# Hyena filters in fewer, wider VectorE operations, and w_out's copy in DRAM issued in the first batch

## The chip, the cores and the metric

One core of one Trainium2 chip. Its engines are TensorE (PE for matmuls, PEld for its weight loads), VectorE (DVE), ScalarE (ACT), GpSimd (POOL) and SyncE (SP, which only issues DMAs here). The metric is the device time of one execution in microseconds (us), lower is better; a kernel's time is the median over its runs.

## The reference, cut to what matters

An encoder layer on two inputs of 1024 tokens × 1024 channels (x_prompt and x_sample), which share all weights. A Fourier branch and a Hyena branch are gated and merged. The Hyena branch multiplies, twice in a row, by a long convolution, whose filter kf is computed from a small network:

```python
    h = (h @ w3.astype(f32)).reshape(L, N_DIR, H_ORDER, H_WIDTH)
    h = h * jnp.exp(-t[:, None, None, None] * jnp.abs(decay.astype(f32))[None])
    h = h / jnp.sum(jnp.abs(h), axis=(0, 1), keepdims=True)
    k = jnp.concatenate([h[:, 0],
                         jnp.zeros((1, H_ORDER, H_WIDTH), f32),
                         h[:L - 1, 1][::-1]], axis=0)
    return jnp.fft.rfft(k, axis=0)
...
    for n, gate in enumerate((x1, x2)):
        z = gate.astype(jnp.float32) * long_conv(z, kf[:, n],
                                                 hyena_d[n].astype(jnp.float32))
    y_h = (z.astype(dt) * jax.nn.silu(hg)) @ w_hyena_out
...
    out = (g_f * y_f + g_h * y_h) @ w_out
    return x + rmsnorm(out, g_post)
```

`x @ w_in` gives all projections (v, x1, x2 and the gates). The filters do not depend on the input, so there are 2 orders × 8 column tiles = 16 of them, computed once and used by both batches.

## The kernel before, in words

**Precision.** Every large product is split: an operand is held as a rounded part and a rest (`wh`/`wl`, `xh`/`xl`, `bh`/`bl`), and one product is three matmuls (`mm3`). All matmuls through `mm` carry line 194 in the profile; DVE and POOL arithmetic through helpers carries lines 177 (`stt`, scalar-tensor-tensor) and 181 (`add`, `sub`, `mul`, the rest of a split), and casts of a split carry line 171.

**Stages.** A Fourier phase runs from 0 to about 250 us. Then come the sixteen filters, between about 230 and 710 us, with gate projections (`spill_gate`) laid between them so that PE has work. Then `branches` runs 32 steps, 16 for each batch, until about 1770 us. The rest, `phase_blocks`, holds the output projections.

**One filter.** `filter_taps` takes column tile ct of order n. For each m of 4 and each i of 2 it makes two matmuls into half of a PSUM tile `pft` (256 columns), an Exp on ACT into `ex` (L640), a product on DVE into `T[i][:, m]`, and an Abs on ACT (L643) into `ex` or, for m = 0, `acc`. DVE adds the Abs values up into `acc`, folds them twice, and a matmul with ones (`pn`, L652 and L653) sums over the partitions. `T0` holds the even row blocks (i = 0), `T1` the odd ones. `filter_spectrum` forms `fE = T0 + T1` and `fO = T0 − T1` (128x1024 each), folds them into `xp` and `xm`, and hands these to `butterfly`, which makes four 128x512 pieces b0 to b3 and splits them into `bh` and `bl`. `forward` multiplies a piece by a table into PSUM (`pXf`). From each group's result DVE and ACT make eight blocks of `kt` (L680 to L698), which SP stores in DRAM as `d_k` (L701, L703).

**The first batch's weights.** `inproj` needs `w_in` in chunks of 128x512 in two parts. SP loads `wr` (L757), ACT casts it to the rounded part (L761) and writes its negative (L762), and POOL issues a DMA that adds the original onto the negative (L763), which leaves the rest. The handle of that DMA is `self.added`. Four places ("rooms") take turns: two pairs `wh`/`wl`, and two tiles `whl` in buffers named draw and draw2. The parts of the three Hyena sections are kept: POOL stores each pair in DRAM as `d_w` (L736), which waits until the accumulating DMA has landed. One chunk serves 24 matmuls `pin`.

**Branches.** Step i computes the projections of step i + 1 and transforms them (`conv_front`, `butterfly`, with the same tile for xp and xm), and then runs `conv_back` for step i: `forward` into `pX`, a product with `k`, loaded from `d_k` by SP (L833) into the two buffers that the filters' `kt` used, giving `t` and `y`, and the inverse transform (`pT`). In the first batch the gate `sg` of a step is read back and passed through Silu on ACT (L1013). In the second batch the weights are read from `d_w` (SP, L754), and a generator, `staging`, advances through POOL: it loads into the rooms draw and draw2, folds, and stores. It waits for `tick`, written by ACT. In its rounds with q = 1 it also issued a transfer in DRAM, eight in all, that brings `w_out` into the layout `d_wo`:

```python
paced = nc.gpsimd.tensor_copy(r[:, 0::2, 0:1], self.tick)
if q == 1:
    i, w = half, (k + 4 * half) * P
    with self.tc.issue_after(paced.ins):
        nc.gpsimd.dma_start(self.d_wo[:, k, 2 * i:2 * i + 2], ...)
```

**Order.** The code is written in the order above, but a scheduler fixes each engine's instruction order at build time, from its own estimates of how long things take. The hardware then keeps that order on each engine and waits where data or a buffer is late.

## Time and profile before

| | |
|---|---|
| time, median of 3 runs | 2428.06 us (2427.44 to 2429.68) |
| profiled execution | 2431.53 us, of which the span is 2429.8 us |
| granted TensorE clock over the span | 0.992 of full |
| busy: PE, DVE, ACT, POOL | 2367.3, 1994.0, 1161.3, 451.1 us |
| DVE in 1250 to 1400 and 1400 to 1550 us | 141.2 and 149.5 of 150 us |
| ACT table loads of 1.28 us, 677 to 693 us | 4 |
| d_wo's transfers issued | 8, of 512 KB each, 1239.2 to 1352.6 us |

A profile is one execution, so its times are a little apart from the median. In lists of waits the columns are the total, the count and the longest; in timelines they are the start, the duration, engine, line, operation and the tiles written and read, and in brackets how long the engine was idle before the instruction and what ended that. Tables by stage give, for each stretch, its length, the busy time of each engine with its instructions, the granted clock, the share of the DMA engines and GB/s.

### The profile page before, as it was taken

The numbers are of one execution on the slowest core, as the hardware profiler recorded it, in microseconds if no ns is written. First come the engines' busy times: TensorE is split into PE (matmuls) and PEld (weight loads), VectorE is DVE, ScalarE is ACT, GpSimd is POOL, SyncE is SP. The second block draws the span as 40 slices with busy tenths as digits, with TensorE's granted clock in tenths as the row PEclk, the third lists the DMA queues.
The fourth block names the chain that finished last, engine by engine and source line by source line (L and its number), as shares of the span: only waits on it lengthen the run. The fifth ranks groups of instructions, "written<-read, shape, count | busy, mean of one in ns | idle before, by whom it ended". The sixth has DMA issues, their size and how long they took to land. (4 is left out here: it accounts for less than half of the span.)

```text
span 2429.8 us, 37269 instructions
## 1 busy us (share of the span) xinstructions
PE 2367.3 (97%) x13006; PEld 2055.2 (85%) x13006; DVE 1994.0 (82%) x3856; ACT 1161.3 (48%) x2208; POOL 451.1 (19%) x575
## 2 busy tenths in 40 slices
PE   6999899999999999999999999999999999999998
PEld 5998788888888888888888888888878888888786
DVE  7785777877777999999899999997666687777777
ACT  5545666666664444444222232333344375656543
POOL 1331111111122222222024554320000000101000
PEclk9999999999999999999999999999999999999999
DMA  7536777887778677766366766554546687888744
GB/s 276 189 124 220 193 197 212 221 212 201 212 218 229 187 201 206 195 184 202 127 225 195 233 210 211 190 174 134 208 149 227 213 300 252 271 269 228 223 157 155
DMA packets 265012, 499.65 MB, mean 206 GB/s; under 512 B 26662, under 2 KB 92423, under 8 KB 264568
## 3 DMA queue, kind: packets, MB, share of 16 engines
q1 hardware_dynamic: 220076, 380.53, 47.9%
q0 software_dynamic: 44560, 116.72, 18.9%
q8 instruction: 102, 1.67, 0.3%
q14 instruction: 86, 0.70, 0.1%
q10 hardware_dynamic: 188, 0.02, 0.0%
HBM read 333.59 MB, written 167.77 MB: 206 GB/s over the span
## 5 line engine op out<-in xcount | busy, mean ns | idle before, releaser
L194 PE MATMUL pin<-xh,wl 128*128 128x512 f32 x1024 | 401.0, 393 | 2.5 <-DMA wl<-d_w 2.5
L194 PE MATMUL pin<-xl,wh 128*128 128x512 f32 x1024 | 402.6, 393 | 0.0
L194 PE MATMUL pin<-xh,wh 128*128 128x512 f32 x1024 | 401.5, 393 | 0.9 <-DMA wh<-d_w 0.9
L194 PE MATMUL pin<-xh,whl 128*128 128x512 f32 x896 | 293.5, 397 | 2.3 <-DMA whl<-in_w_in 2.3
L194 PEld LDWEIGHTS pin<-xh,wl 128*128 128x128 f32 x1024 | 193.4, 189 | 37.9 <-DMA wl<-d_w 2.9
L194 PEld LDWEIGHTS pin<-xh,wh 128*128 128x128 f32 x1024 | 193.3, 189 | 36.5 <-DMA wh<-d_w 1.3
L194 PEld LDWEIGHTS pin<-xl,wh 128*128 128x128 f32 x1024 | 193.4, 189 | 34.4
L194 PEld LDWEIGHTS pin<-xh,whl 128*128 128x128 f32 x896 | 167.6, 190 | 35.5 <-DMA whl<-in_w_in 2.5
L194 PE MATMUL pT<-cinv,yh 128*128 128x256 f32 x1024 | 193.1, 283 | 0.0
L194 PE MATMUL pin<-xl,whl 128*128 128x512 f32 x448 | 177.2, 396 | 0.0
L194 PEld LDWEIGHTS pT<-cinv,yh 128*128 128x128 f32 x1024 | 165.1, 191 | 9.1
L181 DVE TENSOR_TENSOR t<-pX,k 128x1024 f32<-128x1024 f32 x128 | 155.7, 1216 | 13.2 <-PE pX L194 6.2
L194 PE MATMUL pX<-bh,cfwd 128*128 128x256 f32 x768 | 160.8, 286 | 4.2 <-DVE t L181 3.6
L171 ACT CAST yh<-y 128x512 fp32r<-128x512 f32 x128 | 79.3, 619 | 170.1 <-DVE y L181 139.1
L194 PE MATMUL pT<-cinv,yl 128*128 128x256 f32 x512 | 145.7, 285 | 0.0
L171 ACT CAST bh<-b 128x512 fp32r<-128x512 f32 x144 | 88.7, 618 | 98.4 <-DVE b L181 61.2
L194 PEld LDWEIGHTS pX<-bh,cfwd 128*128 128x128 f32 x768 | 126.3, 191 | 8.1 <-DVE t L181 3.9
L181 POOL TENSOR_TENSOR draw<-draw 128x256 f32<-128x256 f32 x96 | 101.7, 1059 | 129.8 <-DMA draw<-d_g 49.9
L181 DVE TENSOR_TENSOR bl<-b,bh 128x512 fp32r<-128x512 f32 x144 | 104.1, 724 | 23.1 <-ACT bh L171 22.9
L194 PE MATMUL pX<-bl,cfwd 128*128 128x256 f32 x384 | 109.9, 286 | 1.4 <-DVE bl L181 1.4
L181 DVE TENSOR_TENSOR yl<-y,yh 128x512 fp32r<-128x512 f32 x128 | 91.0, 711 | 11.1 <-ACT yh L171 10.9
L194 PEld LDWEIGHTS pT<-cinv,yl 128*128 128x128 f32 x512 | 98.1, 192 | 2.0 <-DVE yl L181 0.2
(368 smaller groups left out, 6071.3 us busy)
## 6 DMA issues: line engine op xcount, KB each, us to landing
k<-d_k SPq DMA_DIRECT2D x128, 512.0 KB, 4.4
wr<-in_w_in SPq DMA_DIRECT2D x136, 256.0 KB, 3.3
d_g<-gt SPq DMA_DIRECT2D x92, 256.0 KB, 3.3
d_k<-kt SPq DMA_DIRECT2D x128, 128.0 KB, 3.0
d_k<-kt SPq DMA_DIRECT2D x64, 256.0 KB, 3.5
fz<-d_g SPq DMA_DIRECT2D x64, 256.0 KB, 5.1
wl<-in_w_in POOLq DMA_DIRECT2D x56, 256.0 KB, 5.3
whl<-in_w_in POOLq DMA_DIRECT2D x56, 256.0 KB, 5.4
```

The costliest lines, as they stand in the source:

```text
L171: self.rounded = nc.scalar.copy(h, src)
L181: return e.tensor_tensor(out, a, b, op=op)
L194: return self.nc.tensor.matmul(out, lhsT, rhs, start=start, stop=stop, skip_group_check=shared)
```

## The change

In the filters, each operation works on both halves i of an m, or on both blocks of a pair:

- `T` is laid out by m // 2 instead of by i, so that the product and the Abs take 128x512 at once: 4 of each per filter instead of 8 (the Exp stays at 8).
- `fE` and `fO` are formed in two halves of 128x512 each: first the half of m = 2 and 3, which `db` doesn't enter, then the other.
- `butterfly` writes b1's first two blocks in one operation for filters; for the convolutions two of its operations swap places.
- In the three groups with g ≠ 0, `kt` takes two `stt` of 128x256 instead of one of 128x256 and two of 128x128.
- The eight transfers of `w_out` leave `staging` and stand in steps 1 to 8 of `branches`, each issued by POOL after the last accumulating weight DMA.

```diff
@@ -583,9 +583,12 @@
             de, do, sgn = sm[:, 0, 1], sm[:, 1, 1], 1.0
             se, so = sm[:, 0, 0], sm[:, 1, 0]
         e0, o0, e2, o2 = xm[:, 0, 0], xm[:, 1, 0], xm[:, 0, 2], xm[:, 1, 2]
-        self.stt("dve", b1[:, 0], de, C8, e0)
+        if xm is xp:
+            self.stt("dve", b1[:, 0], de, C8, e0)
+            self.stt("dve", b1[:, 1], se, C8, e2)
+        else:
+            self.stt("dve", b1[:, 0:2], sm[:, 0, ::-1], C8, xm[:, 0, 0:3:2])
         self.stt("dve", b1[:, 3], do, C8 * sgn, o0)
-        self.stt("dve", b1[:, 1], se, C8, e2)
         self.stt("dve", b1[:, 2], so, -C8, o2, MUL, SUB)
         split(1, b1)
         self.stt("dve", b3[:, 0], de, -C8, e0)
@@ -627,7 +630,7 @@
         dec = ws.tile([P, 256], F32, tag="dec", name="dec", bufs=1)
         nc.sync.dma_start(dec, a["filt_decay"][n, ct].partition_broadcast(P))
         nc.scalar.activation(dec, dec, AF.Abs)
-        T = [ws.tile([P, 4, 2, P], F32, tag="x", name=f"T{i}", bufs=4) for i in range(2)]
+        T = [ws.tile([P, 2, 2, 2, P], F32, tag="x", name=f"T{i}", bufs=4) for i in range(2)]
         acc = ws.tile([P, 2, 2, P], F32, tag="yl", name="acc", bufs=2)
         accf = acc.rearrange("p a d c -> p a (d c)")
         for m in range(4):
@@ -638,9 +641,9 @@
                 self.mm(ps[:, i], self.hid[:, q * P:(q + 1) * P], w3h, True, False)
                 self.mm(ps[:, i], self.hid[:, q * P:(q + 1) * P], w3l, False, True)
                 nc.scalar.activation(ex[:, i], dec, AF.Exp, scale=self.vec[:, q:q + 1])
-                Tm = T[i][:, m].rearrange("p d c -> p (d c)")
-                self.mul("dve", Tm, ps[:, i], ex[:, i])
-                nc.scalar.activation(accf[:, i] if m == 0 else ex[:, i], Tm, AF.Abs)
+            Tm = T[m // 2][:, m % 2].rearrange("p i d c -> p i (d c)")
+            self.mul("dve", Tm, ps, ex)
+            nc.scalar.activation(accf if m == 0 else ex, Tm, AF.Abs)
             if m:
                 self.add("dve", accf, accf, ex)
         db = ws.tile([P, P], F32, tag="db", name="db", bufs=1)
@@ -653,16 +656,17 @@
         nc.tensor.matmul(pn[:, P:P + 2], sm, self.ones[:, 0:2], start=True, stop=True)
         nc.vector.reciprocal(self.invn[:, n * 8 + ct:n * 8 + ct + 1], pn[:, P:P + 1])
         self.mul("dve", db, pn[:, 0:P], db)
-        self.stt("dve", T[1][:, 0, 0], db, self.vec[:, 9:10], T[1][:, 0, 0])
-        nc.vector.tensor_scalar(T[0][:, 3, 1], T[0][:, 3, 1], self.vec[:, 8:9], None, op0=MUL)
+        self.stt("dve", T[0][:, 0, 1, 0], db, self.vec[:, 9:10], T[0][:, 0, 1, 0])
+        nc.vector.tensor_scalar(T[1][:, 1, 0, 1], T[1][:, 1, 0, 1], self.vec[:, 8:9], None, op0=MUL)
         return T
 
     def filter_spectrum(self, n, ct, T, ws):
         nc = self.nc
         E = ws.tile([P, 4, 2, P], F32, tag="t4", name="fE", bufs=2)
         O = ws.tile([P, 4, 2, P], F32, tag="t4", name="fO", bufs=2)
-        self.add("dve", E, T[0], T[1])
-        self.sub("dve", O, T[0], T[1])
+        for h in (1, 0):
+            self.add("dve", E[:, 2 * h:2 * h + 2], T[h][:, :, 0], T[h][:, :, 1])
+            self.sub("dve", O[:, 2 * h:2 * h + 2], T[h][:, :, 0], T[h][:, :, 1])
         xp = ws.tile([P, 2, 4, P], F32, tag="q", name="xp", bufs=2)
         xm = ws.tile([P, 2, 4, P], F32, tag="u", name="xm", bufs=1)
         self.add("dve", xp[:, 0], E[:, :, 0], E[:, ::-1, 1])
@@ -679,9 +683,8 @@
 
                 nc.scalar.activation(tmp, X, AF.Copy, scale=th(0))
                 self.stt("dve", kt[:, 0:6:5], X[:, :, 1], th(1), tmp[:, :, 0])
-                self.stt("dve", kt[:, 2], X[:, 1, 0], th(4), tmp[:, 1, 1])
-                self.stt("dve", kt[:, 4], X[:, 0, 0], th(1), tmp[:, 0, 1], MUL, SUB)
-                nc.scalar.mul(kt[:, 1:4:2], kt[:, 0:4:2], -1.0)
+                self.stt("dve", kt[:, 4:2:-1], X[:, :, 0], th(1), tmp[:, :, 1], MUL, SUB)
+                nc.scalar.mul(kt[:, 1:3], kt[:, 0:4:3], -1.0)
             else:
                 for i, pr in enumerate(pairs):
                     R, I = X[:, i, 0], X[:, i, 1]
@@ -965,11 +968,7 @@
                     r = self.stage2.tile([P, 4, 256], F32, tag="draw2", name="draw", bufs=1)
                 else:
                     r = self.cp.tile([P, 4, 256], F32, tag="draw", name="draw", bufs=1)
-                paced = nc.gpsimd.tensor_copy(r[:, 0::2, 0:1], self.tick)
-                if q == 1:
-                    i, w = half, (k + 4 * half) * P
-                    with self.tc.issue_after(paced.ins):
-                        nc.gpsimd.dma_start(self.d_wo[:, k, 2 * i:2 * i + 2], a["w_out"][w:w + P].rearrange("p (n c) -> p n c", n=2))
+                nc.gpsimd.tensor_copy(r[:, 0::2, 0:1], self.tick)
                 for i in range(2):
                     src = {1: self.d_g[0][0], 2: self.d_sh[0]}[q][k + 4 * i] if q < 5 else a["w_out"][(k + 4 * i) * P:(k + 4 * i + 1) * P]
                     nc.gpsimd.dma_start(r[:, 2 * i:2 * i + 2], src.rearrange("p (n c) -> p n c", n=2)[:, :, s])
@@ -1022,6 +1021,10 @@
                 gates(i + 1)
                 if i + 2 < len(steps) and steps[i + 2][0] != steps[i + 1][0]:
                     self.load_x(steps[i + 2][0])
+            if 0 < i <= 8:
+                k, h, w = (i - 1) % 4, (i - 1) // 4, (i - 1) * P
+                with tc.issue_after(self.added.ins):
+                    nc.gpsimd.dma_start(self.d_wo[:, k, 2 * h:2 * h + 2], self.a["w_out"][w:w + P].rearrange("p (n c) -> p n c", n=2))
             y = self.conv_back(n, c, B, ws, stage if b else None)
             B = nxt
             for _ in range({4: 2, 3: 2, 2: 2, 1: 2}.get(len(steps) - i, 0)):
```

Over the whole program DVE has 96 instructions fewer, and ACT five table loads instead of nine. The scheduler's order differs on all engines from about 250 us on; on PE it is the same again from about 1700 us.

**First place: the first filter, about 250 to 270 us.** DVE, with the first filter's acc (acc_3001) and the last pieces of the Fourier phase (fA_2895, fB_2896); first before, then changed:

```order
L657 TENSOR_SCALAR T0_2999<-T0_2999,vec_68 128x128
L181 TENSOR_TENSOR acc_3001<-acc_3001,ex_3028 128x512
L177 SCALAR_TENSOR_TENSOR fA_2895<-pQ_2922,vec_68,fPs_2929 128x255
L181 TENSOR_TENSOR fB_2896<-pQ_2922,fPm_2930 128x255
L177 SCALAR_TENSOR_TENSOR fA_2895<-pQ_2922,vec_68,fPs_2929 128x254
L177 SCALAR_TENSOR_TENSOR fB_2896<-pQ_2922,vec_68,fPm_2930 128x254
L181 TENSOR_TENSOR T1_3000<-pft_3040,ex_3041 128x256
L181 TENSOR_TENSOR w3s_3095<-w3_3092,w3s_3095 128x256
L181 TENSOR_TENSOR acc_3001<-acc_3001,ex_3041 128x512
L181 TENSOR_TENSOR acc_3001<-acc_3001 128x256
L181 TENSOR_TENSOR acc_3001<-acc_3001 128x128
L654 RECIPROCAL invn_72<-pn_3057 128x1
```

```order
L181 TENSOR_TENSOR T1_3000<-pft_3034,ex_3035 128x512
L181 TENSOR_TENSOR w3s_3087<-w3_3084,w3s_3087 128x256
L181 TENSOR_TENSOR acc_3001<-acc_3001,ex_3035 128x512
L660 TENSOR_SCALAR T1_3000<-T1_3000,vec_68 128x128
L181 TENSOR_TENSOR acc_3001<-acc_3001 128x256
L181 TENSOR_TENSOR acc_3001<-acc_3001 128x128
L177 SCALAR_TENSOR_TENSOR fA_2895<-pQ_2902,vec_68,fPs_2909 128x258
L181 TENSOR_TENSOR fB_2896<-pQ_2902,fPm_2910 128x258
L177 SCALAR_TENSOR_TENSOR fA_2895<-pQ_2902,vec_68,fPs_2909 128x258
L177 SCALAR_TENSOR_TENSOR fB_2896<-pQ_2902,vec_68,fPm_2910 128x258
L657 RECIPROCAL invn_72<-pn_3049 128x1
L181 TENSOR_TENSOR db_3045<-pn_3049,db_3045 128x128
```

Before, the group of pQ_2902 stood five rows ahead of these and that of pQ_2922 between the adds. Now all adds of acc stand ahead of both groups, and the group of pQ_2902 lies between them and pn's reciprocal. On ACT, at the cast of a gate's weights (whl_3612 before, whl_3584 now) with the second filter's Exp and Abs around it:

```order
L640 ACTIVATE ex_3105<-dec_3098,vec_68 128x256 x2
L171 CAST w3s_3095<-w3_3092 128x256
L643 ACTIVATE ex_3041<-T1_3000 128x256
L640 ACTIVATE ex_3117<-dec_3098,vec_68 128x256 x2
L761 CAST whl_3612<-wr_3613 128x512
L643 ACTIVATE acc_3103<-T0_3101 128x256
L762 ACTIVATE whl_3612<-whl_3612 128x512
L761 CAST wh_4005<-wr_4007 128x512
L643 ACTIVATE ex_3117<-T0_3101 128x256
L643 ACTIVATE acc_3103<-T1_3102 128x256
```

```order
L646 ACTIVATE ex_3107<-T0_3093 128x512
L646 ACTIVATE ex_3118<-T1_3094 128x512
L171 CAST w3s_3356<-w3_3353 128x256
L643 ACTIVATE ex_3129<-dec_3090,vec_68 128x256 x2
L646 ACTIVATE ex_3129<-T1_3094 128x512
L764 CAST whl_3584<-wr_3585 128x512
L632 ACTIVATE dec_3359<-dec_3359 128x256
L765 ACTIVATE whl_3584<-whl_3584 128x512
L643 ACTIVATE ex_3366<-dec_3359,vec_68 128x256 x2
L643 ACTIVATE ex_3376<-dec_3359,vec_68 128x256 x2
```

Before, the cast (L761) stood behind the second filter's Exp for m = 1, and its negation (L762) behind its first Abs; now the cast (L764) stands behind that filter's last Abs (ex_3129), and the negation (L765) behind the Abs of the next dec.

**Second place: the last filter, about 677 to 693 us.** ACT, with the last filter's Exp and Abs (L640, L643 before) and the first gates' Silu (L1013 before, L1012 now):

```order
L762 ACTIVATE whl_8477<-whl_8477 128x512
L643 ACTIVATE ex_7902<-T0_7886 128x256
L1013 ACT_TABLE_LOAD
L1013 ACTIVATE sg_9173<-sg_9173 128x512
L643 ACTIVATE acc_7888<-T1_7887 128x256
L640 ACT_TABLE_LOAD
L640 ACTIVATE ex_7915<-dec_7883,vec_68 128x256 x2
L1013 ACT_TABLE_LOAD
L1013 ACTIVATE sg_9177<-sg_9177 128x512
L171 CAST bh_7972<-b2_7963 128x512
L761 CAST wh_8700<-wr_8702 128x512
L171 CAST bh_7983<-b1_7964 128x512
```

```order
L804 COPY gt_8206<-pin0_8144 128x512
L804 COPY gt_8209<-pin1_8145 128x512
L764 CAST whl_8319<-wr_8320 128x512
L765 ACTIVATE whl_8319<-whl_8319 128x512
L1012 ACT_TABLE_LOAD
L1012 ACTIVATE sg_9013<-sg_9013 128x512
L1012 ACTIVATE sg_9017<-sg_9017 128x512
L764 CAST wh_8540<-wr_8542 128x512
L765 ACTIVATE wl_8541<-wh_8540 128x512
L1012 ACTIVATE sg_9655<-sg_9655 128x512
```

Now all of the last filter's Exp, Abs and casts bh stand further ahead, and one table load remains at the first Silu.

**Third place: the start of `branches`, about 740 us and on.** SP, with the last filter's stores (d_k1_7) and the first loads of k:

```order
L703 DMA d_k1_7_124<-kt_8618 128x2x128 x2
L701 DMA d_k1_7_124<-kt_8618 128x512
L703 DMA d_k1_7_124<-kt_8641 128x2x128 x2
L833 DMA k_8898<-d_k0_0_109 128x1024
L757 DMA wr_9496<-in_w_in 128x512
L701 DMA d_k1_7_124<-kt_8641 128x512
L833 DMA k_8936<-d_k0_0_109 128x1024
L757 DMA wr_9743<-in_w_in 128x512
L833 DMA k_8975<-d_k0_0_109 128x1024
L833 DMA k_9013<-d_k0_0_109 128x1024
L757 DMA wr_9775<-in_w_in 128x512
```

```order
L706 DMA d_k1_7_124<-kt_8482 128x2x128
L704 DMA d_k1_7_124<-kt_8482 128x512
L706 DMA d_k1_7_124<-kt_8482 128x2x128
L836 DMA k_8738<-d_k0_0_109 128x1024
L760 DMA wr_9215<-in_w_in 128x512
L836 DMA k_8776<-d_k0_0_109 128x1024
L760 DMA wr_9304<-in_w_in 128x512
L760 DMA wr_9337<-in_w_in 128x512
L836 DMA k_8815<-d_k0_0_109 128x1024
L760 DMA wr_9585<-in_w_in 128x512
L836 DMA k_8853<-d_k0_0_109 128x1024
```

On SP the last store now stands ahead of the first load of k. On PE 63 pin matmuls and eight transposes lie between the last pXf and the first pX; before, 17 pin and eight transposes. POOL, around the first of the moved transfers, with the weights of steps 1 and 2:

```order
L736 DMA d_w2_0_1_222<-wl_9101 128x512
L736 DMA d_w2_0_0_221<-wh_9133 128x512
L763 DMA wl_9134<-in_w_in 128x512
L736 DMA d_w2_0_1_222<-wl_9134 128x512
L736 DMA d_w0_2_0_193<-whl_9341 128x512
L763 DMA whl_9341<-in_w_in 128x512
L736 DMA d_w0_2_1_194<-whl_9341 128x512
L736 DMA d_w0_2_0_193<-whl_9373 128x512
```

```order
L739 DMA d_w2_0_1_222<-wl_8941 128x512
L739 DMA d_w2_0_0_221<-wh_8973 128x512
L766 DMA wl_8974<-in_w_in 128x512
L1027 DMA d_wo_246<-in_w_out 128x1024
L739 DMA d_w0_2_0_193<-whl_9182 128x512
L766 DMA whl_9182<-in_w_in 128x512
L739 DMA d_w2_0_1_222<-wl_8974 128x512
L739 DMA d_w0_2_1_194<-whl_9182 128x512
```

The transfer stands right behind an accumulating DMA (wl_8974), and the store that waits for that DMA now stands three rows further on.

## The prediction

> **What bounds the kernel now.** The page's list of engines comes first, for the engine with least room:
>
> ```profile
> PE 2367.3 (97%) x13006; PEld 2055.2 (85%) x13006; DVE 1994.0 (82%) x3856; ACT 1161.3 (48%) x2208; POOL 451.1 (19%) x575
> ```
>
> PE is the bound. Of a span of 2429.8 us it is idle for 2429.8 − 2367.3 = 62.5 us, and the change takes no matmul away. It can therefore gain only what PE waits, or runs at a lower clock, in the stretch whose order it alters (about 250 to 1700 us). The waits of PE that lie in that stretch:
>
> ```profile
> PE pn L652 <- DVE acc L181: 4.3, 2, 4.1
> PE pXf L194 <- ACT bh L171: 3.6, 1, 3.6
> PE pX L194 <- DVE t L181: 3.6, 1, 3.6
> PE pin L194 <- DMA wl<-d_w: 2.5, 1, 2.5
> PE pin L194 <- DMA whl<-in_w_in: 2.3, 1, 2.3
> ```
>
> The columns are total, count, longest. These five make 16.3 us. The table by stage then shows what follows them (second number: PE busy; the last but two: granted clock):
>
> ```profile
> 256.30:263.10 6.80, 4.55 (x14) 3.45 (x14) 5.44 (x12) 2.77 (x6) 1.75 (x3) 0.50 0.57 195
> 266.50:270.00 3.50, 3.49 (x8) 2.83 (x9) 1.89 (x5) 2.55 (x6) 1.31 (x2) 0.51 0.42 92
> 270.00:680.00 410.00, 409.85 (x2219) 354.07 (x2218) 324.60 (x831) 273.75 (x626) 54.47 (x68) 1.00 0.78 211
> 689.80:693.20 3.40, 3.40 (x15) 3.11 (x14) 1.76 (x4) 3.37 (x8) 1.28 (x2) 0.50 0.93 255
> 758.10:761.50 3.40, 3.40 (x16) 3.21 (x17) 2.54 (x4) 2.26 (x5) 0.54 (x1) 0.50 1.03 369
> 900.00:1000.00 100.00, 100.00 (x605) 89.02 (x604) 95.74 (x170) 42.77 (x73) 27.39 (x36) 1.00 0.73 206
> 1345.20:1348.60 3.40, 3.40 (x10) 2.63 (x9) 3.40 (x12) 1.29 (x3) 3.40 (x1) 0.50 0.54 215
> ```
>
> Each of the long waits is followed by about 3.4 us at half clock, so each costs half of that, 1.7 us, on top of itself. In 270 to 680 us, where the sixteen filters run, PE is idle for 410.00 − 409.85 = 0.15 us: nothing is to be had there, whatever the filters save. The second row also gives the pace of back-to-back pin matmuls: 3.49 / 8 = 0.44 us at half clock, 0.22 at full.
>
> [...]
>
> **The change part by part.** *The filters' operations.* The rows of their groups on DVE, then ACT, between 230 and 715 us (busy, mean ns of one):
>
> ```profile
> L181 DVE TENSOR_TENSOR T<-pft,ex 128x256 f32<-128x256 f32 x128 | 50.7, 418 | 14.8 <-PE pft L194 11.6 <-ACT gt L801 1.3 <-ACT ex L640 1.2
> L177 DVE SCALAR_TENSOR_TENSOR kt<-pXf,th,ktmp 128x128 f32<-128x128 f32 x150 | 45.4, 344 | 12.7 <-ACT ktmp L690 11.7 <-PE pin L194 0.7
> L181 DVE TENSOR_TENSOR acc<-acc,ex 128x512 f32<-128x512 f32 x48 | 33.0, 687 | 6.6 <-ACT ex L643 6.3
> L177 DVE SCALAR_TENSOR_TENSOR b<-bs,xm 128x128 f32<-128x128 f32 x120 | 25.5, 285 | 0.0
> L177 DVE SCALAR_TENSOR_TENSOR kt<-pXf,th,ktmp 128x256 f32<-128x256 f32 x45 | 21.6, 480 | 17.1 <-DMA d_k<-kt 9.2 <-ACT ktmp L680 6.0 <-ACT whl L761 1.2
> L181 DVE TENSOR_TENSOR fE<-T,T 128x1024 f32<-128x1024 f32 x16 | 19.5, 1221 | 0.3
> L643 ACT ACTIVATE ex<-T 128x256 f32<-128x256 f32 x96 | 37.7, 414 | 17.9 <-DVE T L181 17.5
> L680 ACT ACTIVATE ktmp<-pXf,th 128x512 f32<-128x512 f32 x45 | 30.5, 683 | 8.2 <-PE pXf L194 8.2
> ```
>
> Per filter on DVE: T, 8 × 0.418 → 4 × 0.687 = −0.60; fE and fO, 2 × 1.22 → 4 × 0.687 = +0.31; b1, 2 × 0.285 → one at 0.480 or less = −0.09; kt in three groups, 3 × (2 × 0.344 − 0.480) = −0.62. Together −1.0 us, 16 us for sixteen filters; since neighbours overlap (128 products of 418 ns fill 50.7 us, not 53.5) I count 10 to 16. ACT: 8 × 0.414 → 4 × 0.683 = −0.58, 9 us in all. On PE's path this is worth 0, covered by the full PE of 270 to 680 us (only if DVE set the pace would it be the 10 to 16). What it does change is how early each filter's chain ends, and with it the order of all engines. So the sum goes by the places.
>
> *A, the first filter (254 to 270 us).* From the timelines of PE, ACT and POOL, and the page's list of DMAs (last number: us to landing):
>
> ```profile
> 258.55 0.79 PE L652 MATMUL pn<-acc,ones 128*128 128x128 f32 x2 [4.13 <-DVE acc L181]
> 266.51 1.22 PE L194 MATMUL pin<-xh,whl 128*128 128x512 f32 x2 [2.34 <-DMA whl<-in_w_in]
> 258.55 0.60 ACT L761 CAST whl<-wr 128x512 fp32r<-128x512 f32 x1
> 261.03 0.61 ACT L762 ACTIVATE whl<-whl 128x512 fp32r<-128x512 f32 x1
> 261.94 0.89 POOL L763 DMA_DIRECT2D whl<-in_w_in  x1 [4.78 <-ACT whl L762]
> wr<-in_w_in SPq DMA_DIRECT2D x136, 256.0 KB, 3.3
> ```
>
> Now the acc adds stand ahead of the last fA/fB group, so pn's 4.1 us go. But late next is the same second whl: its cast now stands behind the second filter's last Abs, its negation behind the following dec Abs, and that last Abs stands behind products that sit behind fA/fB. Counted along DVE from 252.5 us, where the fA/fB group that waits for its store ends now: db's three operations 1.0, a product 0.7, the second group 1.6, two products and two adds 2.7, a split and the last product 1.1, so 259.6; then the Abs and the cast, 1.3, reach 260.9. The next dec has one buffer, which the last Exp reads until about 260; its load then takes some 3.3 us if it is like wr's, issue and Abs about 1. So I put the negation at 264.9 (265.9 if SP is late) instead of 261.03 and, with the 4.6 us from issue to use (261.94 to 266.51), the weights at about 270 instead of 266.5; 0.7 us of pft moves ahead of them. PE waits once, for longer: +2.5 us net, with 0 to +5 as ends.
>
> *B, the last filter (677 to 693 us).* ACT's timeline:
>
> ```profile
> 677.97 1.28 ACT L1013 ACT_TABLE_LOAD   x1
> 682.67 0.63 ACT L1013 ACTIVATE sg<-sg 128x512 f32<-128x512 f32 x1 [3.42 <-DMA sg<-d_g]
> ...
> 687.66 0.60 ACT L171 CAST bh<-b 128x512 fp32r<-128x512 f32 x1
> 691.49 1.28 ACT L640 ACT_TABLE_LOAD   x1
> ```
>
> These are the first and the last of four table loads in 15 us: the last filter's Exp and the first Silu alternate, and ACT waits 3.42 us for a gate while the bh that PE needs stands behind. In the new order all Exp stand ahead of the first Silu, and that spectrum's casts ahead of both. The wait goes with its clock: −3.6 − 1.7 = −5.3 (0 if ACT is late for another reason). Four table loads go, 4 × 1.28 = 5.1 us of ACT, off the path beyond that. Late next is the first v's weights, whose transfers run ahead.
>
> *C, the first inverse transform (748 to 758 us).* SP's and DVE's timelines:
>
> ```profile
> 744.49 0.32 SPq L701 DMA_DIRECT2D d_k<-kt  x1
> 751.44 0.32 SPq L833 DMA_DIRECT2D k<-d_k  x1
> 752.34 5.89 SPq L833 DMA_DIRECT2D k<-d_k  x2
> 756.66 1.23 DVE L181 TENSOR_TENSOR t<-pX,k 128x1024 f32<-128x1024 f32 x1 [4.58 <-DMA k<-d_k]
> ```
>
> The loads of k need buffers that the last filter's stores still hold; between the last pXf and the first pX, PE has only some 17 pin and 8 transposes, about 5 us. Now there are 63 pin and the transposes, about 15 us at 0.22 each, and the chain above (744.5 to 756.6) takes 12. So −3.6 − 1.7 = −5.3 too, half of it if the chain slips by 4 us.
>
> *w_out's transfers.*
>
> ```profile
> L972 POOL DMA_DIRECT2D d_wo<-in_w_out x8: 554/554/587, 1239.2 to 1352.6; - x8
> ...
> DMA to landing us min/median/max: 3.6/7.1/9.5
> POOL d_w L736 <- DMA wl<-in_w_in: 108.8, 22, 7.3
> ...
> 707.50 0.89 POOL L763 DMA_DIRECT2D whl<-in_w_in  x1
> ...
> 719.79 0.90 POOL L763 DMA_DIRECT2D wl<-in_w_in  x1
> ```
>
> Eight issues of 0.55 us move from 1239–1353 to steps one to eight of the first batch. There each stands behind an accumulating weight transfer and mostly ahead of a d_w store that waits for that transfer anyway (108.8 us of such waits in 22 stores), so the issue costs 0; without that cover it would be 8 × 0.55 = 4.4 us of POOL. The 512 KB beside the weights may delay them: 0 as long as the four weight rooms hold. In the second batch (D) the one 2.5 us wait for wl, at 1342 us, lies among the removed transfers; but eight of them gave one such wait, so it may as well belong to the order: I give half of 2.5 + 1.7, −2, with 0 and −4 as ends. POOL's own row there is off the path.
>
> *Sum.* +2.5 − 5.3 − 5.3 − 2 = −10.1. The static order is new over 1400 us, and an order that meets the chip anew finds some wait of its own: +2, against the 16.3 that the old one has. That is −8 on the profiled execution (2429.8 + 1.7 outside = 2431.5): 2423.5. The median of the runs, 2428.06, is 3.5 below that execution; 2428.1 − 8 = **2420**.
>
> **The rivals.** (1) *The stalls only move.* For it: PE's order was made by estimates of durations, and five long waits in 1400 us show how often these miss. Against: B and C have causes that can be named, and the new order removes both. B and C are made up by others: 2426 to 2430, say 2428.
>
> (2) *The weight chain becomes the bound (slower).* Its place is POOL at 710 to 960 us: store, accumulate, wait, store. From the first to the third of three accumulates, a kept chunk takes (719.79 − 707.50) / 2 = 6.1 us there; PE eats one in 24 × 0.22 = 5.3 us where no transforms lie between. A pure run of pin, longer now (about 55 us, ten chunks), eats 0.8 us per chunk, 8 in all, and four rooms hold about that: 4 × 5.3, less 5.3 for the one in use and 8.0 from cast to use (258.55 to 266.51), is 7.9; the 512 KB behind each accumulate, 7.1 us to landing, then makes the next chunk late. It decides where two accumulates in a row are late by over 4 us; each stall costs 2 to 3 us and 1.7 of clock, and three of them 12 to 14, so −8 becomes +5: 2433 (with A at its worse end, 2436). Against it: with transforms between, PE never waited in the row for 900 to 1000 us, so the slack was not touched there.
>
> [...]
>
> (3) *All the places come good.* A loses both waits (−6.4 in place of +2.5), D goes wholly with its clock (−4.2 in place of −2): 11 less, 2409.
>
> **How the numbers follow.** Forecast 0.50; rival (1) 0.25; rival (2) 0.17; rival (3) 0.08. The likeliest is 2420; its own range, from A's ends and half of C or D, is 2415 to 2425. To hold 8 in 10 the range takes in (1) and the lower part of (2): 2411 to 2434. About 0.2% (4.9 us) is what a measurement of this kernel can tell from no change. Faster by more (below 2423.2): most of the forecast and all of (3), 0.53. Within: (1) and the forecast's upper edge, 0.28. Slower: (2) and a rest of (1), 0.19.
>
> **What would show it.** Right: no table load between the first Silu and the last Exp, five in all; no PE wait at pXf on bh, nor at the first pX on t; pn without a wait, and one wait for whl of 5 to 9 us near 262 to 270; DVE busy 10 to 16 us less, with PE's busy time about the same. Wrong: PE waits for wl or whl between 710 and 960 us, each with a stretch at half clock behind it; or waits of pX and pin at new places that together reach 10 us.

## The result and the profile after

The changed kernel took 2422.61 us (median of 20 runs, 2416.75 to 2427.35), the kernel before 2429.69 us in 20 runs beside it: 0.9972 of it, 95% interval [0.9965, 0.9979], or 7 us less. The forecast was 8 us less. Its profiled execution took 2420.15 us, 2.5 below its median, while that of before lay 1.8 above; so the two profiles differ by 11.4 us, and what they show has to be read against the 7 of the runs. The page's list of engines after:

```profile
PE 2360.6 (98%) x13006; PEld 2050.7 (85%) x13006; DVE 1976.0 (82%) x3760; ACT 1147.7 (47%) x2140; POOL 447.5 (19%) x575
```

DVE has 18.0 us less, ACT 13.6. PE is idle for 57.7 us instead of 62.5. The operations cost what the rows of before said (table of groups on DVE, 230 to 715 us; busy, mean ns):

```profile
L181 DVE TENSOR_TENSOR T<-pft,ex 128x512 f32<-128x512 f32 x64 | 43.1, 684 | 6.7 <-PE pft L194 6.0 <-ACT ex L643 0.4
L177 DVE SCALAR_TENSOR_TENSOR kt<-pXf,th,ktmp 128x256 f32<-128x256 f32 x92 | 40.1, 477 | 11.7 <-ACT ktmp L684 5.8 <-DMA d_k<-kt 5.7
L181 DVE TENSOR_TENSOR fE<-T 128x512 f32<-128x512 f32 x32 | 22.0, 687 | 0.4
```

Where the change can act on time, in the stretch from the end of the Fourier phase (its last pse) to the first pg of the output projections, the table by stage has these rows, of before and of after (length, PE busy, and so on):

```profile
222.78:1766.95 1544.17, 1524.89 (x8674) 1335.98 (x8673) 1326.69 (x2636) 696.52 (x1388) 354.21 (x435) 0.99 0.67 198
```

```profile
221.94:1756.48 1534.54, 1518.79 (x8673) 1332.24 (x8672) 1309.16 (x2540) 683.25 (x1320) 350.67 (x435) 0.99 0.67 199
```

The stretch is 9.6 us shorter: 3.5 us of PE's idle time and 6.1 of its busy time are gone. The number of matmuls is the same; the busy time falls mostly because less of it lies at half clock (4.3 of the 6.1 us, by the table of places below). The waits of PE in that stretch after:

```profile
PE pin L194 <- DMA whl<-in_w_in: 4.5, 1, 4.5
PE pin L194 <- ACT whl L764: 3.6, 1, 3.6
PE pT L194 <- ACT yh L171: 2.7, 1, 2.7
PE tph L824 <- ACT T1s L875: 2.2, 1, 2.2
PE pft L194 <- DVE T L181: 1.4, 1, 1.4
PE pX L194 <- ACT bh L171: 0.9, 1, 0.9
```

The waits of pXf on bh (B), of the first pX on t (C) and of pin on wl in the second batch (D) are gone. The first filter (A) has three waits, 9.5 us, where it had two of 6.5; new are 2.7 us at 993 us and 2.2 at 1520. The next table sums it up by place. Half clock is half of PE's busy time in the pieces that the trace shows at half clock, worked out from the records of its matmuls; in the kernel before, one pin follows another there by 0.43 us, and by 0.23 at full clock.

| from the end of the Fourier phase | before: idle, half clock | after: idle, half clock | difference |
|---|---|---|---|
| to 300 us (A) | 6.6, 4.0 | 9.5, 3.1 | +2.0 |
| 300 to 720 (B) | 3.8, 1.7 | 0, 0 | −5.5 |
| 720 to 1100 (C) | 4.2, 1.7 | 3.6, 0 | −2.2 |
| 1100 to the first pg (D) | 4.8, 1.7 | 2.6, 1.7 | −2.2 |
| sum | 28.4 | 20.6 | −7.8 |

A further 1.8 us of the 9.6 is in neither column; it stays open. One execution says little of a single place: in the kernel before and in e5 below, whose order is the same on all engines from 800 us on, idle time and half clock in the row of D make 6.5 and 4.0 us. At A, the eight profiles with the order of before there (before, e2, e4, e5 and e9 to e12) give 9.7 to 12.9 us, and the four with the order of the change (after, e1, e7 and e8) 11.9 to 13.8.

At B, ACT after has one table load where four stood, and PE is fully busy in both rows that held B and C:

```profile
685.66 1.28 ACT L1012 ACT_TABLE_LOAD   x1 [0.42 <-DMA sg<-d_g]
```

```profile
620.00:700.00 80.00, 80.00 (x382) 66.88 (x381) 38.67 (x87) 36.87 (x69) 15.53 (x21) 1.00 0.76 206
700.00:800.00 100.00, 100.00 (x568) 87.49 (x567) 74.23 (x137) 45.56 (x82) 31.38 (x46) 1.00 0.83 240
```

At A, the timelines of PE, ACT and POOL show the late weights, as the prediction counted them, but the negation some 2 us earlier:

```profile
261.31 0.80 PE L194 MATMUL pin<-xh,whl 128*128 128x512 f32 x1 [3.62 <-ACT whl L764]
267.90 1.22 PE L194 MATMUL pin<-xh,whl 128*128 128x512 f32 x2 [4.51 <-DMA whl<-in_w_in]
260.65 0.60 ACT L764 CAST whl<-wr 128x512 fp32r<-128x512 f32 x1
262.39 0.42 ACT L632 ACTIVATE dec<-dec 128x256 f32<-128x256 f32 x1 [1.14 <-DMA dec<-in_filt_decay]
262.72 0.61 ACT L765 ACTIVATE whl<-whl 128x512 fp32r<-128x512 f32 x1
263.63 0.89 POOL L766 DMA_DIRECT2D whl<-in_w_in  x1 [6.36 <-ACT whl L765]
```

### The profile page after: what moved, and what is told of

It is laid out like the page before. It is cut to its first block, busy times and chain, and to the rows that moved or that the text cites. A ratio compares the mean times of both kernels' runs of the same rounds, so it can differ in the third digit from the quotient of the medians.

```text
span 2418.3 us, 37119 instructions
## 1 busy us (share of the span) xinstructions
PE 2360.6 (98%) x13006; PEld 2050.7 (85%) x13006; DVE 1976.0 (82%) x3760; ACT 1147.7 (47%) x2140; POOL 447.5 (19%) x575
## 5 line engine op out<-in xcount | busy, mean ns | idle before, releaser
L194 PEld LDWEIGHTS pT<-cinv,yh 128*128 128x128 f32 x1024 | 165.4, 191 | 12.9 <-ACT yh L171 3.2
L181 POOL TENSOR_TENSOR draw<-draw 128x256 f32<-128x256 f32 x96 | 93.8, 977 | 112.1 <-DMA draw<-in_w_out 39.5
L181 DVE TENSOR_TENSOR bl<-b,bh 128x512 fp32r<-128x512 f32 x144 | 100.3, 703 | 11.5 <-ACT bh L171 11.4
```

The lines of the kernel that those rows point to most:

```text
L181: return e.tensor_tensor(out, a, b, op=op)
L194: return self.nc.tensor.matmul(out, lhsT, rhs, start=start, stop=stop, skip_group_check=shared)
```

## The experiments

Three theories stood against each other. *Places*: the gain is the waits at B and C with their half clock, taken away by another order of the engines. *Work*: it is the work that VectorE and ScalarE save. *Transfers*: it is w_out's transfers that leave the second batch. For each run the table gives the ratio to the kernel before in runs beside it, and the length of the stretch from the last pse to the first pg in its profile, with idle time and half clock as above.

| run | ratio, 95% interval | stretch | idle, half clock |
|---|---|---|---|
| before | 1 | 1544.2 | 19.3, 9.1 |
| changed kernel | 0.9972 [0.9965, 0.9979] | 1534.5 | 15.8, 4.8 |
| e1 filters alone | 0.9980 [0.9967, 0.9994] | 1539.9 | 17.4, 7.5 |
| e2 transfers alone | 1.0014 [0.9999, 1.0028] | 1550.0 | 23.5, 11.2 |
| e3 same work, other order | 0.9997 [0.9981, 1.0012] | 1540.5 | 19.2, 5.7 |
| e4 kt and b1 alone | 0.9995 [0.9983, 1.0008] | 1543.5 | 19.2, 9.1 |
| e5 Silu behind Exp | 0.9964 [0.9950, 0.9977] | 1534.6 | 12.6, 6.4 |
| e6 weights first | 0.9979 [0.9966, 0.9992] | 1538.3 | 17.2, 4.6 |
| e7 transfers beside filters | 0.9973 [0.9961, 0.9984] | 1537.9 | 16.8, 7.1 |
| e8 two transfers a step | 0.9968 [0.9955, 0.9981] | 1535.1 | 15.3, 4.2 |
| e9 Silu, transfers in steps | 0.9963 [0.9951, 0.9975] | 1535.0 | 13.7, 5.8 |
| e10 Silu, transfers beside filters | 0.9959 [0.9948, 0.9971] | 1535.1 | 12.4, 7.3 |
| e11 Silu, wider kt | 0.9957 [0.9945, 0.9969] | 1535.4 | 14.2, 4.9 |
| e12 Silu, kt, transfers beside filters | 0.9954 [0.9940, 0.9967] | 1533.2 | 13.6, 3.3 |

One thousandth is 2.4 us.

The last column answers to the times: for each of the thirteen kernels, idle time and half clock together fall against the kernel before (28.4 us) by an amount that lies inside the interval of its measured time. VectorE's saving does not: e4 saves 12.0 us of it and is 1.2 us faster, e5 saves 1.4 and is 8.7 faster.

**e1, the filters alone.** The changed kernel, with w_out's transfers left in `staging`:

```diff
-            if 0 < i <= 8:
-                k, h, w = (i - 1) % 4, (i - 1) // 4, (i - 1) * P
-                ...
...
+                if q == 1:
+                    i, w = half, (k + 4 * half) * P
+                    ...
```

> The filters' edits alone, w_out's transfers left in the second batch. Places theory (the gain is the waits before the last filter's pXf and before the first pX, with the half clock behind each): both waits gone, five table loads, 5 to 8 us below the kernel before. Transfer theory (the gain is the moved transfers): within 2 us of the kernel before. Work theory (the gain is the 10 to 16 us of VectorE and the 14 us of ScalarE that are saved): also 5 to 8 us below, so this run only splits the first two.

It is 4.9 us below the kernel before (1.5 to 8.0). B and C are gone. Within the intervals the whole gain of the change lies in the filters' edits. The transfer theory's 2 us are just inside this interval; together with e2, where the transfers alone gain nothing, it is out.

**e2, the transfers alone.** The kernel before, with the transfers in steps 1 to 8 and out of `staging`; no filter edit:

```diff
-                if q == 1:
-                    i, w = half, (k + 4 * half) * P
-                    ...
...
+            if 0 < i <= 8:
+                k, h, w = (i - 1) % 4, (i - 1) // 4, (i - 1) * P
+                ...
```

> w_out's transfers moved to the first batch, filters as before. Places theory: the waits at the last filter's pXf (3.6 us) and at the first pX (3.6 us) stay, nine table loads; the wait for wl at 1342 us may go, so 0 to 4 us below the kernel before. Transfer theory: 5 us or more below.

It came out 3.4 us above the kernel before (−0.2 to 6.8): neither theory's value. The wait for wl at D is gone as hoped, but PE's waits elsewhere grew:

```profile
PE pX L194 <- DVE t L181: 6.5, 1, 6.5
PE pn L652 <- DVE acc L181: 5.1, 1, 5.1
PE pX L194 <- ACT bh L171: 4.9, 1, 4.9
```

C has 6.5 us instead of 3.6, and the wait of pX on bh near 830 us, 0.6 in the kernel before, is 4.9. On PE, VectorE and SyncE the order is that of the kernel before until 1283 us, so the same order gave both 3.6 and 6.5 us at C. Whether the transfers as such did this was left to e8 to e10.

**e3, the same work in another order.** The kernel before; the two products and Abs of one m are only written behind both halves' matmuls and Exp:

```diff
             for i in range(2):
                 ...
                 nc.scalar.activation(ex[:, i], dec, AF.Exp, scale=self.vec[:, q:q + 1])
+            for i in range(2):
                 Tm = T[i][:, m].rearrange("p d c -> p (d c)")
                 self.mul("dve", Tm, ps[:, i], ex[:, i])
                 nc.scalar.activation(accf[:, i] if m == 0 else ex[:, i], Tm, AF.Abs)
```

> The kernel before with the same operations and widths; only the two products and two Abs of one m are written after both halves' matmuls and Exp, not half by half. VectorE has as many instructions as before. Its order has one table load at the first Silu and 63 pin between the last pXf and the first pX, as in the changed kernel. Places theory: both waits gone, 5 to 9 us below the kernel before, though no work is saved. Work theory: within 2 us of the kernel before, since VectorE's busy time is the same. Luck theory (any new order gains or loses at random): anything within 10 us, with waits at other places making up the sum.

No operation is saved, and yet the order is that of the changed kernel at B and C: both waits are gone. But the time is only 0.7 us below (−2.9 to 4.6), a miss for the places theory as I had sized it. The waits of this run show where it went:

```profile
PE pin L194 <- DMA whl<-in_w_in: 6.0, 2, 5.7
PE pin L194 <- ACT whl L762: 3.3, 1, 3.3
PE pT L194 <- ACT yh L171: 2.4, 1, 2.4
...
PE pXf L194 <- ACT bh L171: 1.9, 1, 1.9
PE pn L653 <- DVE acc L181: 1.3, 2, 1.1
```

A costs more than in the kernel before (10.1 us of waits and 2.3 of half clock, 6.6 and 4.0 there), and the pXf wait of 1.9 us is a new one, among the filters at 455 us, with half clock behind it. There bh stands behind an Abs on ScalarE that waits for its small load, and not behind work of VectorE:

```profile
454.40 0.42 ACT L629 ACTIVATE dec<-dec 128x256 f32<-128x256 f32 x1 [2.87 <-DMA dec<-in_filt_decay]
```

The stretch is still 3.6 us shorter than before; in this execution the part ahead of it was 1 us shorter and the part behind it 2 us longer. A new order removes the old waits and brings others; the net is smaller than the two waits taken out.

**e4, the wider kt and b1 alone.** The kernel before, with these two edits of the change (shortened; b1's `if` and kt's negation go with them):

```diff
-                self.stt("dve", kt[:, 2], X[:, 1, 0], th(4), tmp[:, 1, 1])
-                self.stt("dve", kt[:, 4], X[:, 0, 0], th(1), tmp[:, 0, 1], MUL, SUB)
+                self.stt("dve", kt[:, 4:2:-1], X[:, :, 0], th(1), tmp[:, :, 1], MUL, SUB)
...
+            self.stt("dve", b1[:, 0:2], sm[:, 0, ::-1], C8, xm[:, 0, 0:3:2])
```

> Of the filters' edits only the wider kt and b1 operations: 0.7 us of VectorE saved per filter, 11 us in all, which is most of what the change saves there. Its order keeps nine table loads and some 17 pin between the last pXf and the first pX. Places theory: both waits stay, within 2 us of the kernel before. Work theory: 4 to 6 us below.

1.2 us below (−1.9 to 4.1): 12 us of VectorE less (1982.0 of 1994.0 in the profiles), and B and C stand, 3.1 and 4.0 us. The work theory's 4 to 6 us touch this interval only at its end; in the form that VectorE's time is what is gained, it is as good as out for these operations, and e11 adds to that.

**e5, Silu behind Exp.** The kernel before, with one constraint and nothing else:

```diff
-                nc.scalar.activation(ex[:, i], dec, AF.Exp, scale=self.vec[:, q:q + 1])
+                self.lastexp = nc.scalar.activation(ex[:, i], dec, AF.Exp, scale=self.vec[:, q:q + 1])
...
-                    nc.scalar.activation(sg, sg if early else ps[q], AF.Silu)
+                    with tc.issue_after(self.lastexp.ins):
+                        nc.scalar.activation(sg, sg if early else ps[q], AF.Silu)
```

> The kernel before with one constraint more: every Silu of the first batch is ordered behind the last filter's last Exp on ScalarE. Table loads fall from nine to five; some 20 rows of PE stay between the last pXf and the first pX. If the alternating tables and the wait for the gate were what kept bh late, the 3.6 us wait at the last filter's pXf goes with its 1.7 us of half clock and the rest of the changed stretch stays: 3 to 6 us below the kernel before. If the last filter was late for another reason, the wait stays and the time is within 2 us of before.

8.7 us below the kernel before (5.6 to 12.1), more than expected and about as much as the whole change. Its waits:

```profile
PE pn L652 <- DVE acc L181: 3.9, 1, 3.9
PE pin L194 <- DMA whl<-in_w_in: 3.1, 1, 3.1
PE pin L194 <- DMA wl<-d_w: 2.3, 1, 2.3
PE pX L194 <- DVE t L181: 1.6, 1, 1.6
PE pX L194 <- ACT bh L171: 1.2, 1, 1.2
```

B is gone, and C fell from 3.6 us with half clock behind it to 1.6 without, although PE has as few rows between the last pXf and the first pX as before. ScalarE's order differs from that of before from 678 us on, that of the other engines only from about 695, behind B; so for B it is the order of Silu and Exp that counts.

For C more has changed than that. In the order of before, SyncE's last store of d_k stands behind the first load of k. In e5, as in the changed kernel, the scheduler put it ahead of that load, and the next load starts 3 us behind the store, not 7 as in the prediction's rows (744.49 and 751.44):

```profile
739.07 0.44 SPq L701 DMA_DIRECT2D d_k<-kt  x1
739.68 0.33 SPq L833 DMA_DIRECT2D k<-d_k  x1
742.11 4.23 SPq L833 DMA_DIRECT2D k<-d_k  x2
```

In the three kernels with the store behind the load (before, e2 and e4) the wait C is 3.6 to 6.5 us; in the other eleven it is 0 to 1.8. It is not simply B's delay handed on: in e2, B is 1.7 us without half clock, and C is 6.5. No run changed SyncE's order alone, so this cause of C is argued, not shown.

Which of the two parts of B counted, the table loads or the wait for the gate, e5 does not separate, since it removes both. The kernels that keep all four loads say something of the second: where the first Silu waits 3.42, 3.23 and 1.59 us for its gate (before, e4 and e2), PE waits 3.61, 3.15 and 1.73 us. So the wait for the gate reaches PE nearly one for one; what the loads add on the same queue, no run shows alone.

**e6, weights first.** The changed kernel, the first gates emitted before the second filter's taps, and (`negs` holds the negations in the order in which they are written)

```diff
+            with self.tc.issue_after(self.negs[3].ins) if (n, ct) == (1, 0) and m else ExitStack():
                 nc.scalar.activation(accf if m == 0 else ex, Tm, AF.Abs)
```

> The changed kernel with the second gate's second weights (cast and negation on ScalarE) ordered ahead of the second filter's Abs for m = 1 and on. If those weights are what PE waits for at 257 to 268 us (3.6 and 4.5 us, 3 us of half clock), both waits together fall from 8.1 to 2 to 4 us: 3 to 6 us below the changed kernel, which is 10 to 13 below the kernel before. If the weights' buffer is held by the Fourier phase's last pieces until about 257 us in any case, it is under 2 us.

5.1 us below the kernel before (1.9 to 8.3), so no gain on the changed kernel. The wait for the cast fell from 3.6 to 1.0 us, but that for the landing is 4.9: PE only reached it earlier (262.31 instead of 267.90 us). Two new waits of pn, 1.1 and 1.0 us, came among the filters. The 3 to 6 us that I expected are not there.

**e7 and e8, where the transfers stand.** The changed kernel with the transfers issued beside filters 4 to 11 (e7, first), or two at once in steps 1 to 4 (e8):

```diff
-            if 0 < i <= 8:
-                k, h, w = (i - 1) % 4, (i - 1) // 4, (i - 1) * P
...
+                if 4 <= i < 12:
+                    k, h, w = (i - 4) % 4, (i - 4) // 4, (i - 4) * P
```

```diff
-            if 0 < i <= 8:
-                k, h, w = (i - 1) % 4, (i - 1) // 4, (i - 1) * P
+            if 0 < i <= 4:
+                for j in (2 * i - 2, 2 * i - 1):
+                    k, h, w = j % 4, j // 4, j * P
```

> The changed kernel with w_out's eight transfers issued beside filters 4 to 11 (about 330 to 550 us), where PE never waits and GpSimd stores no weights. PE's order differs from the changed kernel's in a few dozen rows. If the transfers cost something beside the first batch (the stores behind them on GpSimd, and the gate products behind the stores), this is 1 to 4 us below the changed kernel; if they are free there, within 2 us of it, and the wait at 993 us stays.

> The changed kernel with two transfers of 512 KB in each of steps 1 to 4 instead of one in each of steps 1 to 8; all engines but GpSimd keep their order. If a transfer delays the accumulating weight DMA ahead of it and so the store and the gate product behind it, two at once delay them by 4 us or more and PE waits anew between 730 and 860 us: 2 to 6 us above the changed kernel. If PE only loses through its own static order, within 2 us of it.

Both lie on the changed kernel's ratio (0.9973 and 0.9968 beside 0.9972). Two transfers at once brought no wait of weights and no slower time; the wait at 993 us, 2.96 us in e7 and 2.58 in e8, does not depend on them; e1 and e3, which leave the transfers in the second batch, have it too (2.5 and 2.4 us).

**e9 and e10, the transfers on the order of e5.** e5's edit, with the transfers in steps as in e2's diff (e9) and beside filters as in e7's (e10). All engines but GpSimd, and one Silu on ScalarE, have the same order in both.

> The kernel before with Silu ordered behind the last Exp, and w_out's transfers moved to steps 1 to 8 as in the change; no filter edit. The order is that of the run with the Silu alone up to the second batch. If the transfers beside the first batch cost nothing, the waits of that batch stay as they were there (about 3 us) and the wait for wl at 1336 us (2.3 us and 1.7 of half clock) goes: 8 to 13 us below the kernel before. If the transfers delay the stores and gate products on GpSimd, a wait of several us comes at about 830 us as in the run with the transfers alone: 2 to 7 below.

> The same, with w_out's transfers beside filters 4 to 11. TensorE, VectorE and SyncE have the order of the run with the transfers in steps; only GpSimd's differs. If the transfers are free in the steps, the two are within 2 us of each other; if they cost something there, this one is 3 us or more below it. In either case 8 to 13 us below the kernel before.

They are 9.0 and 10.0 us below the kernel before, and their stretches are 1535.0 and 1535.1 us: the place of the transfers makes no difference. Both have lost the wait for wl at D, and both have the wait of pX on bh at 830 us, 4.7 and 4.9 us, which e5 had with 1.2. I had expected that wait from transfers beside the first batch; e10 has none near it and the same wait, so they are not needed for it, and presumably not in e2 either. What goes with it, the timelines of POOL, DVE and ACT show, e5 first, then e10:

```profile
816.16 0.56 POOL L736 DMA_DIRECT2D d_w<-whl  x1 [4.96 <-DMA whl<-in_w_in]
816.73 4.03 POOL L181 TENSOR_TENSOR x<-x,sg 128x512 f32<-128x512 f32 x2
823.64 1.28 DVE L181 TENSOR_TENSOR eo<-x 128x512 f32<-128x512 f32 x2
```

```profile
818.61 0.56 POOL L736 DMA_DIRECT2D d_w<-whl  x1 [6.62 <-DMA whl<-in_w_in]
819.18 6.06 POOL L181 TENSOR_TENSOR x<-x,sg 128x512 f32<-128x512 f32 x2
822.92 2.88 DVE L181 TENSOR_TENSOR eo<-x 128x512 f32<-128x512 f32 x2
826.21 0.63 ACT L1014 ACTIVATE sg<-sg 128x512 f32<-128x512 f32 x1 [5.84 <-DMA sg<-d_g]
```

In e10 the two gate products on GpSimd overlap with two adds on VectorE, and both take longer than in e5: 6.06 us for the products (4.03 in e5, where they end before the adds start, and 2.54 at this place in the kernel before), 2.88 instead of 1.28 for the adds. The products hold the buffers that SyncE needs for the next gate; the Silu at the head of ScalarE waits 5.84 us for it, and bh stands behind. That the products wait for the store ahead of them (6.62 us here, 4.96 in e5) is how a weight that lands 1.7 us later grows to a wait of 5 on PE. The new wait at 993 us in the changed kernel ends in a like chain: there the products take 5.31 us, and ScalarE waits 10.42 us for the gate.

In e9, where the products and the two adds overlap as well, they take 5.88 and 2.88 us. But the products also vary without these adds beside them, from 2.54 to 4.03 us above, and in the changed kernel the two adds that start 1 us into the 5.31 us of the products (yc, at 984.69 us) take 1.29. No run took one of the two away, so what makes them longer is not shown.

**e11 and e12, on top of the Silu.** e5's edit with e4's (e11), and both with the transfers beside filters as in e7's diff (e12).

> The kernel before with Silu ordered behind the last Exp and with the wider kt and b1 operations, which save 11 us of VectorE. Work theory: 4 us or more below the run with the Silu alone, so 12 or more below the kernel before. Places theory: nothing on top of the Silu, 6 to 11 below the kernel before.

> The kernel before with Silu ordered behind the last Exp, the wider kt and b1, and w_out's transfers beside filters 4 to 11. Places theory: the second batch's wait for wl (3.1 us in the run with Silu and kt) goes, and the wait for bh at 830 us grows to 4 or 5 us if the gate products on GpSimd fall on VectorE's eo again, or stays at 1: 9 to 15 us below the kernel before, no more than 4 from the runs with two of the three. Work theory: the gains add up, 15 us or more below.

e11 is 10.4 us below the kernel before (7.5 to 13.4), e5 8.7: no separable gain from the wider operations, with which VectorE is busy 7 us less in the profiles (1985.5 of 1992.6). e12 is 11.2 below (8.0 to 14.6), with the shortest stretch of all, 1533.2 us. It lies ahead of the changed kernel (6.8 below, 5.1 to 8.5), though the intervals overlap at the ends.

## Why the prediction was right, and where it was not

- **What bounds the kernel.** Right. 18 us of VectorE and 14 us of ScalarE went and bought nothing where PE was full: 300 to 680 us is fully busy before and after (379.85 and 380.00 of 380.00 us), and e4 and e11 show no gain from VectorE's saving that can be told from none.
- **The operations' costs.** Right for the durations (684, 477 and 687 ns, from rows of 687, 480 and 687). The sum was low: 10 to 16 us, measured 18.0.
- **A, +2.5.** Measured +2.0 in waits and half clock, not far outside what A varies by with one order. The mechanism was the one named, but the negation came at 262.72 us and not 264.9, and PE's wait is split in three. Its size agrees partly by chance. e6 could not turn it into a gain.
- **B, −5.3.** The wait and its clock went, 3.6 and 1.7 us, and e5 shows why: the order of Silu and Exp on ScalarE alone does it.
- **C, −5.3.** The wait is gone, but the cause was not quite mine. I put it down to the distance of 63 pin on PE; e5 keeps the short distance, 17 pin, and loses more than half of the wait with all its half clock. What e5 shares with the changed kernel is SyncE's last store ahead of the first load of k. In the changed kernel both hold, so which of them took the wait away there stays open.
- **w_out's transfers, −2.** Wait D went whole with its clock, −4.2, the far end of the forecast. It went in every run that moved the transfers and stayed in e4, e5 and e11; in e1 and e3, which left them, it was gone as well. So the transfers in the second batch are a part of it, but not its only cause. In the first batch they cost nothing that can be measured (e8, e9 beside e10). Rival (2), the weight chain as the bound, did not occur.
- **New waits, +2.** Under-sized. The new ones at 939, 993, 1155 and 1520 us make 6.2 us and 1.7 of half clock; small waits of the old order, 2.9 us, went, which leaves +5. The place that I missed is the gate product on GpSimd: I named the store behind the weight, not what stands behind the store.
- **The sum.** −8 forecast, −7 measured. A, B and C came near their sizes; D took 2 us more and the new waits gave back 3 more than forecast, and that these two nearly cancel is luck.

So what the change gains is waits of PE and the half clock behind them. One part of it, the last Exp ahead of the first Silu, gave about as much alone when e5 put it into the kernel before by one constraint; another way of writing the filters made the scheduler choose the same. That this order is all of the change's gain is not shown: e3 has it too, without any saving, and is only 0.7 us below the kernel before (−2.9 to 4.6), as 5 us of new waits and half clock came among its filters. The changed kernel has none there; whether it owes that to the wider operations or to the luck of its order, no run separates.

## What to carry to other kernels

Where one engine is full, look for the few places where it waits, follow each back to the instruction at the head of the waiting queue, and try that one ordering constraint alone before rewriting the work: here one such line gave as much as the whole change. With a scheduler that fixes the order, any edit to the program gives a new order with waits of its own, so compare the sum of PE's waits and of its half clock, not the work saved, and take single places from more than one execution: here they varied by 2 to 3 us with no change of order. And name, for each wait, everything that stands behind it on its queue, one link further than the first.

## What was not expected of the hardware

In these traces the length of a wait of PE does not settle whether half clock follows; what goes with it is how the wait lies on a grid. In all fourteen the records of the granted clock change only on a grid of 3.413 us: the distances between changes are multiples of it to within 2 ns. In e3 a wait of 1.95 us at 455 us lies in one window of that grid, and the next window runs at half clock; in e11 one of 3.06 us at 1340 us is cut by the grid into 1.86 and 1.20 us, and no half clock follows (tables by stage, cut at the grid; the first two numbers are the length and PE's busy time, the last but two the clock):

```profile
451.98:455.40 3.42, 1.47 (x11) 0.99 (x9) 3.29 (x14) 1.00 (x3) 0.00 (x0) 1.00 0.34 99
455.40:458.81 3.41, 3.41 (x9) 2.74 (x10) 2.47 (x5) 3.41 (x10) 0.51 (x1) 0.50 0.25 80
```

```profile
1335.05:1338.47 3.42, 1.56 (x8) 0.99 (x6) 3.42 (x6) 0.00 (x0) 0.00 (x0) 1.00 0.99 340
1338.47:1341.88 3.41, 2.21 (x10) 1.83 (x11) 3.41 (x14) 1.24 (x2) 2.33 (x1) 1.00 0.81 317
1341.88:1345.29 3.41, 3.41 (x21) 3.02 (x20) 2.29 (x3) 1.81 (x4) 3.17 (x4) 1.00 0.27 72
```

With PE's records of all fourteen traces cut at their grids, from 230 us on, every window at full clock in which PE was idle for 1.88 us or more was followed by one at half clock, and none in which it was idle for less than 1.80 us; between the two, both occurred. In the kernel before the nearest on the two sides are 1.89 us (the window from 252.90 us), with half clock behind it, and 1.68 (from 682.98), without. So the wait of 1.95 us in e3 came with a window at half clock behind it, and the one of 3.06 in e11 with none. The changed kernel has both cases: 2.19 us at 1520 us with half clock behind it, and 2.75 us at 993 us, cut into 1.87 and 0.88, without.

From 230 us to the first pg the pieces at half clock are one or two windows long in the kernel before (3.413 and 6.827 us) and one or four in the changed one (3.413 and 13.653). By the count of half of PE's busy time, each window costs up to 1.7 us, which can be more than half as much as the wait before it: 1.7 behind 2.49 us at 1345 us in the kernel before, and 1.7 behind 2.19 at 1520 us in the changed one.
